# A hybrid mixer layer on one core: the passage from the output projection to the up products rebuilt, weight sums of three pairs made in memory, down products issued by parts

## The chip, the cores and the metric

One core of a Trainium2 chip runs the whole layer in one launch. The metric is the device time of one execution in microseconds (us). The engines are TensorE (PE in the profile), VectorE (DVE), ScalarE (ACT), GpSimd (POOL) and SyncE (SP, which issues DMAs; POOL issues some too). Each engine works through its own instructions in order.

## The reference, cut to what matters

The layer runs over 640 tokens: 512 denoising tokens and 128 context tokens, 1024 features each, with adaLN scale and shift (`sc2`, `sh2`) that differ between the two sets. What the change touches is its second half:

```
x = x + g1 * (merged @ w_o)
h = rmsnorm(x, norm2_g) * (1.0 + sc2) + sh2
z = dwconv3(h @ w_up, cw, cb)            # w_up: 1024 x 5632
a, g = split(z, 2)
x = x + g2 * ((silu(g) * a) @ w_down)    # w_down: 2816 x 1024
```

followed by a final `rmsnorm`. All of it is float32. The kernel splits each operand into a rounded high part and a low rest (`hi`, `lo`), and one product becomes three matmuls: high by high, high by low and low by high.

## The kernel before, in words

The up and the down products use a seven-product form of a 2 x 2 block product. The operand `h` is cut in two token halves (c = 0, 1, 320 tokens each) and two feature halves (q = 0, 1, 512 features each): a11, a12 (c = 0), a21, a22 (c = 1). The weights of one *pair* (a 128-column tile of each half of `w_up`; there are 22 pairs) have four blocks b11, b21, b22, b12. The products are numbered 1 to 7: 1 and 2 use a11 and a12 as they are; 5, 6 and 7 use a21 - a22, (a21 - a22) - a11 and a11 - a21; 4 uses a22; 3 uses a12 + (operand 6). On the weight side, three sums of blocks (`S0`, `S1`, `S2`) go with 6 or 5 or 7, a fourth sum (`S3`) with product 4 and b22 with product 3. One product is 12 matmuls of 128 x 128 by 128 x 320 (4 chunks of 128 features, three parts each).

*The passage.* `wo_tile` makes the output projection tile by tile. After its last tile it takes the statistics of half 0, normalises (`normed`), adds the shift (`shifted`), and splits into high and low (`part`), for the feature halves in turn. `up_all` then starts the pairs 0 to 3 (`BRIDGE = 4`) with their products 1 and 2, which need half 0 only, and beside them does half 1: statistics (`stats_a` to `stats_d`), `normed` and `shifted` of both feature halves, and then `operands()`, which forms the operands of products 5, 6, 7, 4 and 3, one after the other on VectorE (differences and low parts) and ScalarE (high parts, line 138 in the profile, as for every engine wrapped by `Ordered`). Then `up_pair(0)` to `up_pair(22)` run as a pipeline: `up_pair(p)` makes products 6, 5 and 7 of pair p and 4 and 3 of pair p - 1, the convolution and the gate of pair p - 2 (`taps`, `gate`, `gated`, `keep`), and prepares the weights of pair p + 1 (`up_ah`/`up_al` for b11 and b21, `up_sums`, `up_b`/`up_bl`, and in the next pair `up_c`).

*Buffers.* Raw weights wait in a pool of three tiles (`rp`, tag `raw`); from pair 3 on, the second half of an odd pair goes to the region `G`. Half 1 lies in the region `X1`, half 0 in `XL1`; the operands go to `B`, `A`, `D`, `XL0` and `XL1`. The low parts of S3 and b22 are made by `low_dma`: ScalarE writes the negated high part and a DMA of GpSimd's queue adds the raw block to it.

*The down part.* `down_all` works through 42 groups (7 products by 6 chunks) of 24 matmuls (12 for the last chunk). Each needs `w_hi`, `w_lo`, `x_hi` and `x_lo` of its group; group i's are prepared some groups ahead.

*What sets the order.* With `fixed[0]` set, the instructions of VectorE, ScalarE and GpSimd that go through `ovec`, `oact` and `opool` keep the program's order. Matmuls and SyncE's DMAs are not held: a planner orders them at compile time by its own costs. Generators put in with `start` are stepped along as the program issues matmuls (`tick`); `up_early` and the sums of `w_down` in memory (`weight_sums`) run beside earlier stages.

Of the kernel before, what the change touches and what calls it, by code (L numbers as in the profile page):

```python
# [57 lines left out]
def tile_step(ctx: ExitStack, tc: tile.TileContext, a: dict, outs: list, dbg=None):  # L58
# [1112 lines left out]
    axs = [None]  # L1171
    x2d = dram.tile([2, P, 4, T], F32, name="x2d")
    KO = ((0, 1, 4, 5), (2, 3, 6, 7))
    HOLD = 5
# [67 lines left out]

    def shifted(c, q, on_vec):
        f = hh[c][:, q]
        for k in range(4):
            for (t0, t1, v) in pieces(c):
                x, sh = f[:, k, t0:t1], modt[:, 24 + 4 * q + k, v:v + 1]
# [25 lines left out]
    def wo_tile(n, w):  # L1273
# [152 lines left out]

    def up_b(p_):
        s = sums(p_)
        b = up[p_, "B"] = unit(p_, 1)
        c = up[p_, "C"] = unit(p_, 2)  # L1430
        oact(b[:, 0:2], s[:, 0:2], AF.Copy)
        oact(b[:, 4], s[:, 2], AF.Copy)
        return b, c

    def up_bl(p_):
        s, b, c = sums(p_), up[p_, "B"], up[p_, "C"]
        ovec.tensor_tensor(b[:, 2:4], s[:, 0:2], b[:, 0:2].bitcast(F32), ALU.subtract)
        ovec.tensor_tensor(c[:, 4], s[:, 2], b[:, 4].bitcast(F32), ALU.subtract)

    def up_c(p_, r):  # L1440
        c = up[p_, "C"]
        for i, x in enumerate((sums(p_)[:, 3 + p_ % 2], r[1][:, 0])):
            oact(c[:, i], x, AF.Copy)
            low_dma(c[:, 2 + i].rearrange("p b c -> p (b c)"), x.rearrange("p b c -> p (b c)"))

    def prod(o, p_, i, first, part=None):

        u, ih, il = PROD[i]
        wh = up[p_, u][:, ih]
        wl = up[p_, "C" if i == 7 else u][:, il]  # L1450
        xh_, xl_ = fx["x"][i]
        for k in range(4) if part is not None else ():
# [101 lines left out]
    def up_pair(p_, r):  # L1554
# [4 lines left out]
        if p_ == 0:  # L1559
            prod(up[p_, "b"][1], p_, 5, True)  # L1560
            up_u2(p_)
            first_sum(2)
        if o >= 0:
            taps(o, 1)
        if q >= 0:

            oact(tmp(2), up[q, "b"][0], AF.Copy)
            for (i0, i1, c) in S2:
                ovec.tensor_tensor(ubuf(q, 1)[:, c:c + i1 - i0], up[q, "b"][1][:, i0:i1], tmp(2)[:, i0:i1],
                                  ALU.subtract)  # L1570
# [6 lines left out]
        if o >= 0:  # L1577
# [5 lines left out]
        if inner and p_:  # L1583
            up_c(p_, r[p_])
        if o >= 0:
            keep(o)
        if inner:
            if p_ + 2 < NPAIR:
                r[p_ + 2] = up_load(p_ + 2)
            elif p_ + 2 == NPAIR:  # L1590
                down_start(0)
        else:
            prep([1], [1])
        if q >= 0:
# [7 lines left out]
            if p_ == 1:  # L1602
                first_copy(3)
                first_sum(3)
        if inner and p_:
            up_u2(p_)
        if q >= 0:

            prod(up[q, "b"][1], q, 3, False)
            ovec.tensor_tensor(ubuf(q, 1)[:, 1:1 + HC], up[q, "b"][1], tmp(q % 2), ALU.subtract)  # L1610
        if nx:
            up_b(n)
        if not inner:
            prep([2], [])
        if q >= 0:
            centre(q, 1)
        if not inner:
            prep([], [2])
        if nx:
            up_bl(n)  # L1620
        if inner:
            b1, b2 = up[p_, "b"]
            if p_:
# [5 lines left out]
    def operands():  # L1629
        t = region("X0", [P, 2, 4, HC])  # L1630
        t5, t6 = t[:, 0], t[:, 1]
        a11, a12, a21, a22 = [hh[c][:, q] for c in range(2) for q in range(2)]
        x4, x6, x5, x7 = [region(t_, [P, 2, 4, HC], F32R) for t_ in ("XL0", "A", "B", "D")]
        fx["x"].update({i: (x[:, 0], x[:, 1]) for i, x in ((6, x6), (5, x5), (7, x7), (4, x4))})

        def lo(x, v):
            ovec.tensor_tensor(x[:, 1], v, x[:, 0].bitcast(F32), ALU.subtract)

        ovec.tensor_tensor(t5, a21, a22, ALU.subtract)
        oact(x5[:, 0], t5, AF.Copy)  # L1640
        ovec.tensor_tensor(t6, t5, a11, ALU.subtract)
        oact(x6[:, 0], t6, AF.Copy)
        lo(x5, t5)
        ovec.tensor_tensor(a21, a11, a21, ALU.subtract)
        oact(x7[:, 0], a21, AF.Copy)
        lo(x6, t6)
        oact(x4[:, 0], a22, AF.Copy)
        lo(x7, a21)
        ovec.tensor_tensor(t5, a12, t6, ALU.add)
        lo(x4, a22)  # L1650
        x3 = region("XL1", [P, 2, 4, HC], F32R)
        oact(x3[:, 0], t5, AF.Copy)
        lo(x3, t5)
        fx["x"][3] = x3[:, 0], x3[:, 1]

    def up_all(_):
# [4 lines left out]
        r = {1: up_load(1)}  # L1661
        up_sums(1, r[1], 0)
        up_sums(1, r[1], 1)
        fixed[0] = True
# [4 lines left out]
        for p_ in range(BRIDGE):  # L1669
# [6 lines left out]
            if p_ == 0:  # L1676
                stats_a(1, g[0][:, 1])
                dg = stats_b(1, g[0][:, 1])
            if p_ == 1:
                stats_c(dg, g[1][:, 1])  # L1680
                for q in range(2):
                    normed(1, q, g[1][:, 1])
                shifted(1, 0, False)
                shifted(1, 1, True)
# [5 lines left out]
        operands()  # L1690
        for p_ in range(NPAIR + 1):
            up_pair(p_, r)
        taps(NPAIR - 1, 1)
        gate(NPAIR - 1)
# [96 lines left out]
    def prep(iw, ix):  # L1791
        for f, l in ((w_hi, iw), (x_sum, ix), (w_lo, iw), (x_hi, ix), (x_lo, ix)):
            for i in l:
                f(i)

# [12 lines left out]
    def group_mm(o, i, js):  # L1808
        p_, g = GR[i]
        w, s = slots["w", i], slots["x", i]  # L1810
        for kk in range(many(g)):
            k = 2 * g + kk
            for j in js:
                for q, (h, x) in enumerate(((0, 0), (0, 1), (1, 0))):
                    mm(o[j], w[:, h, kk, j * P:(j + 1) * P], s[:, x, kk, :],  # L1815
                       start=(p_ in STARTS and k == 0 and q == 0), stop=(k == 10 and q == 2),
                       skip_group_check=True)
                tick(0.44)

# [413 lines left out]
```

## Time and profile before

| | us |
|---|---|
| median of 3 runs | 1040.14 (1038.79 to 1040.32) |
| profiled execution, its time | 1039.98 |
| its span, first to last instruction | 1038.2 |
| PE busy in the span | 1016.9 (98%) |
| DVE, ACT, POOL busy | 824.9, 541.3, 129.9 |

The profiled execution lies 0.16 us below the median. 1.8 us of its time lie outside the span. PE is busy in 98% of the span and not busy for 21.3 us of it.

### The profile page before, as it was taken

How to read it: one execution, taken by the hardware profiler on the slowest of the kernel's cores; microseconds unless marked ns; L12 is line 12 of the kernel's file. 1: busy time of each engine (PE TensorE's matmuls, PEld its weight loads, DVE VectorE, ACT ScalarE, POOL GpSimd, SP SyncE). 2: the span in 40 equal slices, each digit the busy share in tenths (PEclk: the TensorE clock that was granted, in tenths of full speed). 3: DMA queues.
4: the chain of work that ended last, by engine and by line, in shares of the span. 5: the costliest groups of instructions: out<-in, count | busy, mean ns of one | idle time of the engine just before them, and what ended most of it. 6: DMA issues, size and time to landing. Idle time of an engine off the chain costs nothing. (4 is left out here: it accounts for less than half of the span.)

```text
span 1038.2 us, 19770 instructions
## 1 busy us (share of the span) xinstructions
PE 1016.9 (98%) x8020; PEld 989.7 (95%) x8020; DVE 824.9 (79%) x1333; ACT 541.3 (52%) x926; POOL 129.9 (13%) x195
## 2 busy tenths in 40 slices
PE   8999999999999999999999998999999999999996
PEld 6899989998899999999999988999999999899996
DVE  5658899789878677767669578998888886998775
ACT  6532343342332554445446357777777776655663
POOL 2000010201100011111110001222222222000000
PEclk9999989999999999999999999999999999999998
DMA  9854443464154277898778652765565657976732
GB/s 362 325 198 127 128 136 123 133 217 130 54 201 179 89 236 203 259 257 231 199 222 318 255 178 68 195 167 148 149 157 159 160 154 210 355 266 183 226 92 102
DMA packets 64541, 196.00 MB, mean 189 GB/s; under 512 B 9121, under 2 KB 22049, under 8 KB 61121
## 3 DMA queue, kind: packets, MB, share of 16 engines
q1 hardware_dynamic: 49008, 149.08, 41.4%
q0 software_dynamic: 15440, 45.65, 19.1%
q8 instruction: 63, 1.03, 0.4%
q14 instruction: 30, 0.24, 0.1%
HBM read 160.72 MB, written 44.56 MB: 198 GB/s over the span
## 5 line engine op out<-in xcount | busy, mean ns | idle before, releaser
L305 PE MATMUL g<-XH,w 128*128 128x320 f32 x832 | 202.7, 319 | 0.0
L305 PEld LDWEIGHTS g<-XH,w 128*128 128x128 f32 x832 | 144.0, 191 | 2.6 <-issue 1.4
L305 PE MATMUL g<-XL,w 128*128 128x320 f32 x416 | 130.5, 314 | 0.0
L305 PEld LDWEIGHTS g<-XL,w 128*128 128x128 f32 x416 | 79.4, 191 | 0.8 <-issue 0.7
L138 ACT ACTIVATE w<-F 128x1024 fp32r<-128x1024 f32 (+1 forms) x65 | 49.0, 788 | 23.7 <-issue 18.0
L270 ACT ACTIVATE w<-raw 128x1024 fp32r<-128x1024 f32 (+1 forms) x34 | 37.8, 1113 | 36.2 <-PE g L305 14.0
L271 DVE TENSOR_TENSOR w<-raw,w 128x1024 fp32r<-128x1024 f32 (+1 forms) x34 | 43.7, 1285 | 8.1 <-ACT w L270 7.9
L138 DVE TENSOR_TENSOR w<-F,w 128x1024 fp32r<-128x1024 f32 (+1 forms) x43 | 41.9, 997 | 8.1 <-ACT w L138 7.8
L1056 PE MATMUL m<-XH,w 128*128 128x320 f32 x192 | 45.1, 310 | 0.0
L1815 PE MATMUL m<-XH,w 128*128 128x320 f32 x264 | 41.4, 312 | 1.7 <-DVE XH L138 0.9
L138 DVE SCALAR_TENSOR_TENSOR X<-MG,p2t,X 128x641 f32<-128x641 f32 x44 | 38.9, 884 | 5.0 <-ACT X L138 4.1
L138 DVE TENSOR_TENSOR w<-S,w 128x1024 fp32r<-128x1024 f32 (+1 forms) x32 | 32.2, 1021 | 13.3 <-ACT w L138 12.4
L138 ACT ACTIVATE w<-S 128x1024 fp32r<-128x1024 f32 (+1 forms) x32 | 28.0, 894 | 26.7 <-issue 12.5
L1815 PEld LDWEIGHTS m<-XH,w 128*128 128x128 f32 x264 | 38.9, 188 | 2.8 <-DVE XH L138 1.4
L938 POOL DMA_DIRECT2D wsum<-in_w_down_dram x24 | 19.9, 903 | 160.2 <-DMA wsum<-in_w_down_dram 95.3
L138 DVE SCALAR_TENSOR_TENSOR X<-X,p2t,X 128x641 f32<-128x641 f32 x44 | 38.9, 884 | 1.0
L1815 PE MATMUL m<-XL,w 128*128 128x320 f32 x264 | 39.6, 309 | 0.0
L1459 PE MATMUL g<-XL,C 128*128 128x320 f32 x240 | 38.6, 309 | 0.4 <-ACT MG L138 0.4
L1815 PEld LDWEIGHTS m<-XL,w 128*128 128x128 f32 x264 | 38.9, 188 | 0.0
L1459 PE MATMUL g<-XL,w 128*128 128x320 f32 x240 | 38.7, 310 | 0.0
L1459 PEld LDWEIGHTS g<-XL,C 128*128 128x128 f32 x240 | 36.0, 188 | 0.7 <-ACT MG L138 0.7
L1459 PEld LDWEIGHTS g<-XL,w 128*128 128x128 f32 x240 | 35.9, 188 | 0.4 <-ACT MG L138 0.3
(552 smaller groups left out, 2808.4 us busy)
## 6 DMA issues: line engine op xcount, KB each, us to landing
raw<-in_w_up_dram SPq DMA_DIRECT2D x32, 512.0 KB, 5.1
raw<-in_w_gp_dram SPq DMA_DIRECT2D x18, 640.0 KB, 6.9
wsum<-in_w_down_dram POOLq DMA_DIRECT2D x20, 512.0 KB, 7.9
raw<-in_w_in_dram SPq DMA_DIRECT2D x19, 512.0 KB, 4.4
H<-in_w_adt_dram SPq DMA_DIRECT2D x14, 512.0 KB, 4.2
actd<-X POOLq DMA_DIRECT2D x22, 256.0 KB, 4.2
raw<-in_w_gate_dram SPq DMA_DIRECT2D x8, 640.0 KB, 4.0
wsum<-in_w_down_dram SPq DMA_DIRECT2D x10, 512.0 KB, 7.0
```

Source lines behind the costliest of these rows:

```text
L138: r = f(*args, **kw)
L270: act(w[:, 0], raw, AF.Copy)
L271: low = lambda: vec.tensor_tensor(w[:, 1], raw, w[:, 0].bitcast(F32), ALU.subtract)
L305: mm(o, w[:, h, k0 + k, :], r(k)[:, s], start=(k == 0 and i == 0), stop=(k == kt - 1 and i == 2))
L938: tc.keep_in_program_order(eng.dma_start(o, x, **kw))
L1056: mm(o, w[:, k, :], x[:, k, :], start=(first and k == 0 and j == 0), stop=(k == 3 and j == 2), skip_group_check=True)
L1459: mm(o, w[:, k, :], x[:, k, :], start=(first and k == 0 and j == 0), stop=(k == 3 and j == 2), skip_group_check=True)
L1815: mm(o[j], w[:, h, kk, j * P:(j + 1) * P], s[:, x, kk, :], start=(p_ in STARTS and k == 0 and q == 0), stop=(k == 10 and q == 2), skip_gro ...
```

## The change

Four edits belong together. (1) *Half 1 is normalised as a difference.* While the statistics of half 1 are on their way, VectorE subtracts the scaled halves (`diff`); after that `normed` of the first feature half gives a21 - a22 at once, with the difference of the shifts (`dsh`, made once) added. The operands are then formed in place by a generator, `operands(m)`, whose steps are called between the products. (2) *A new order* in `up_all` and in `up_pair` 0 to 2; the shifts of half 0 go half to VectorE and half to ScalarE, those of a22 to ScalarE; products of pairs 0 and 1 issue all four high-by-high matmuls first. (3) *Weight sums of pairs 1 to 3 are made in memory* by `up_sums_ahead`, 24 DMAs of 256 KB (12 of SyncE, 12 adding ones of GpSimd), started after the input projection's section `du`; `up_load` of these pairs fetches the sums, and their `up_sums` fall away. (4) *Down products by parts*: a group issues high by high, then low weights, then low operand, and group 3's high parts are prepared before the last convolution.

The core of the diff (left out: signatures, `down_start`, moved lines of `up_pair` that only mirror others):

```diff
+            if sec == "du":
+                start(up_sums_ahead(), 6)
...
+    def up_sums_ahead():
+        b11, b21, b22, b12 = [a["w_up"][1:BRIDGE, h, :, i] for h in range(2) for i in range(2)]
+        s = [usum[:, :, 4 * i:4 * i + 4] for i in range(4)]
...
+        for steps in (((nc.sync, 0, b11), (nc.sync, 2, b12)), ((pool, 0, b12), (pool, 2, b22)),
+                      ((nc.sync, 1, s[0]),), ((pool, 1, b22),), ((nc.sync, 3, s[1]),), ((pool, 3, b21),)):
+            for eng, i, x in steps:
+                put(eng, s[i], x, **({"accum_op": ALU.add} if eng is pool else {}))
+            yield 12
...
         for q in range(2):
             normed(0, q, rb)
-            shifted(0, q, False)
+            shifted(0, q, (0, 1), True)
+            shifted(0, q, (2, 3), False)
+        for q in range(2):
             part(xw[:, 2 * q], xw[:, 2 * q + 1], hh[0][:, q])
...
     def up_load(p_):
+        if p_ < BRIDGE:
+            u = usum[p_ - 1].rearrange("p (i k) c -> p i k c", i=4)
+            r = [rp.tile([P, 2, 4, P], F32, tag="raw", name=nm("raw")) for _ in range(2)]
+            nc.sync.dma_start(r[0], u[:, 0:2])
+            nc.sync.dma_start(r[1][:, 1], u[:, 2])
+            nc.sync.dma_start(sums(p_)[:, 3 + p_ % 2], u[:, 3])
+            nc.sync.dma_start(r[1][:, 0], a["w_up"][p_, 1][:, 0])
+            return r
...
+        if p_ < 2:
+            for j, (w, x) in enumerate(((wh, xh_),) + (((wl, xh_), (wh, xl_)), ((wh, xl_), (wl, xh_)))[p_]):
+                for k in range(4):
+                    mm(o, w[:, k, :], x[:, k, :], ...)
...
     def up_pair(p_, r):
+        if q >= 0:
+            u = tmp(2) if q else gp.tile([P, HC], F32, tag="gt", name=nm("u"))
+            oact(u, up[q, "b"][0], AF.Copy)
...
+            if q == 0:
+                up_c(1, r[1], (0,))
+                up_u2(1)
+                up_c(1, r[1], (1,))
+                next(fx["op"])
+                up_bm(1, r[1])
+                next(fx["op"])
+        if o == 0:
+            first_copy(3)
+            first_sum(3)
         if o >= 0:
             taps(o, 1)
...
-        if nx and p_:
+        if nx and n >= BRIDGE:
             up_sums(n, r[n], 0)
             up_sums(n, r[n], 1)
...
+            if p_ == 1:
+                up_b(2, r[2])
+                up_bl(2, r[2])
             centre(q, 0)
-            taps(q, 0)
+            if p_ > 1:
+                taps(q, 0)
+        if o == 0:
+            gate(0)
+            gated(0)
+            keep(0)
...
+    def diff(ks):
+        a, b = hh[1][:, 0, ks[0]:ks[-1] + 1], hh[1][:, 1, ks[0]:ks[-1] + 1]
+        ovec.tensor_tensor(a, a, b, ALU.subtract)
+
+    def operands(m):
+        (a11, a12), (t5, a22) = [[hh[c][:, q] for q in range(2)] for c in range(2)]
+        t6, t7 = a11, t5
+        normed(1, 0, m)
+        shifted(1, 0, (0, 1), True, dsh)
+        shifted(1, 0, (2, 3), False, dsh)
+        normed(1, 1, m)
+        l5 = operand(5, t5, "B")
+        yield
+        shifted(1, 1, range(4), False)
+        ovec.tensor_tensor(t6, t5, a11, ALU.subtract)
+        l6 = operand(6, t6, "A")
+        l5()
+        yield
+        ovec.scalar_tensor_tensor(t7, t6, -1.0, a22, ALU.mult, ALU.subtract)
+        l7 = operand(7, t7, "D")
+        l6()
+        l4 = operand(4, a22, "XL0")
+        l7()
+        l4()
+        yield
+        ovec.tensor_tensor(t5, a12, t6, ALU.add)
+        yield
+        l3 = operand(3, t5, "XL1")
+        l3()
+        yield
...
+                diff(range(3))
+                stats_s(1, g[0][:, 1])
+                diff((3,))
+                dg = stats_d(1)
...
             up_pair(p_, r)
+        prep_head()
         taps(NPAIR - 1, 1)
...
+    def prep_head():
+        for f in (w_hi, x_sum, x_hi):
+            f(HEAD)
...
-        for kk in range(many(g)):
-            k = 2 * g + kk
-            for j in js:
-                for q, (h, x) in enumerate(((0, 0), (0, 1), (1, 0))):
+        for q, (h, x) in enumerate(((0, 0), (1, 0), (0, 1))):
+            for kk in range(many(g)):
+                k = 2 * g + kk
+                for j in js:
```

`operand(n, x, tag)` writes the high part of operand n at once (ScalarE) and returns the call that makes its low part (VectorE). `up_bm` is the last line of the old `up_bl` (the low part of S2).

## Rows read from the trace of the kernel before

**Rows 1.** Stages: busy us of each engine (instructions), granted clock, DMA share, GB/s
```profile
140.00:240.00 100.00, 99.99 (x927) 94.71 (x926) 85.80 (x180) 40.17 (x89) 13.39 (x14) 0.97 0.48 151
600.00:643.00 43.00, 36.97 (x234) 35.21 (x233) 35.33 (x48) 27.17 (x49) 3.79 (x18) 0.96 0.39 121
```

**Rows 2.** Waits of PE, whole span: waiter, releaser: total us, times, longest
```profile
PE g L1459 <- ACT MG L138: 3.1, 2, 2.6
...
PE g L1459 <- DVE B L138: 1.2, 1, 1.2
...
PE g L1459 <- DVE XH L138: 1.0, 1, 1.0
PE m L1815 <- DVE XH L138: 0.9, 2, 0.5
PE g L1459 <- DVE A L138: 0.8, 1, 0.8
PE m L1815 <- ACT XH L138: 0.6, 1, 0.6
```

**Rows 3.** Stages of 2 us in the passage, columns as in rows 1
```profile
630.00:632.00 2.00, 2.00 (x9) 2.00 (x9) 2.00 (x3) 0.95 (x2) 0.29 (x7) 0.50 0.00 0
```

**Rows 4.** Order of time, PE: start, us, instruction, count, idle before and releaser
```profile
620.60 0.42 PE L1459 MATMUL g<-B,E 128*128 128x320 f32 x1
...
629.54 0.65 PE L1459 MATMUL g<-D,E 128*128 128x320 f32 x2 [2.64 <-ACT MG L138]
...
642.43 1.92 PE L1459 MATMUL m<-A,E 128*128 128x320 f32 x12
```

**Rows 5.** Order of time, DVE and ACT in the passage
```profile
612.58 2.88 DVE L138 TENSOR_TENSOR X<-X,g 128x1280 f32<-128x1280 f32 x2 [0.92 <-PE g L1226]
...
614.10 2.67 ACT L138 ACTIVATE X<-X,modt 128x192 f32<-128x192 f32 x8 [2.56 <-DVE X L138]
615.50 1.79 DVE L138 TENSOR_SCALAR X<-X,modt 128x192 f32<-128x192 f32 x8
...
619.26 1.28 ACT L138 ACTIVATE B<-X 128x1280 fp32r<-128x1280 f32 x1 [2.17 <-DVE X L138]
...
627.89 1.27 ACT L138 ACTIVATE XL<-X 128x1280 fp32r<-128x1280 f32 x1 [1.80 <-DVE X L138]
629.06 0.42 ACT L138 ACTIVATE MG<-g 128x320 f32<-128x320 f32 x1
```

**Rows 6.** Groups by form, 603 to 660: instruction, count, busy us, mean ns
```profile
L138 DVE SCALAR_TENSOR_TENSOR X<-MG,p2t,X 128x641 f32<-128x641 f32 x5 | 4.4, 886 | 1.8 <-ACT X L138 1.6
...
L138 DVE TENSOR_TENSOR X<-XL,X 128x1280 f32<-128x1280 f32 x2 | 3.0, 1486 | 0.0
...
L138 DVE TENSOR_TENSOR w<-F,w 128x1024 fp32r<-128x1024 f32 x2 | 2.4, 1216 | 0.0
...
L138 DVE TENSOR_TENSOR F<-F,raw 128x512 f32<-128x512 f32 x5 | 3.4, 687 | 0.1
```

**Rows 7.** Order of time, ACT and PE at pairs 2 to 4
```profile
643.09 1.28 ACT L138 ACT_TABLE_LOAD   x1
...
644.48 0.74 ACT L138 ACTIVATE X<-X 128x641 f32<-128x641 f32 x1
...
652.13 1.05 ACT L138 ACTIVATE MG<-raw 128x1024 fp32r<-128x1024 f32 x1
...
658.69 0.60 PE L1459 MATMUL g<-XH,MG 128*128 128x320 f32 x3
659.13 1.92 PE L1459 MATMUL m<-D,w 128*128 128x320 f32 x12
```

**Rows 8.** DMA issues, 590 to 660: tile, queue, count, KB each, median us to landing
```profile
raw<-in_w_up_dram SPq DMA_DIRECT2D x5, 512.0 KB, 5.0
...
C<-raw POOLq DMA_DIRECT2D x1, 256.0 KB, 5.9
```

**Rows 9.** Order of time, ACT where the down part begins
```profile
895.64 0.74 ACT L138 ACTIVATE X<-X 128x641 f32<-128x641 f32 x1 [2.61 <-DVE X L138]
```

More of the change, by code (lines that the diff above doesn't have):

```diff
@@ L929, in tile_step, with flat, put @@
     wsum = dram.tile([4, P, 11, 512], F32, name="wsum")
+    usum = dram.tile([BRIDGE - 1, P, 16, P], F32, name="usum")
+    def up_sums_ahead():
+        b11, b21, b22, b12 = [a["w_up"][1:BRIDGE, h, :, i] for h in range(2) for i in range(2)]
+        s = [usum[:, :, 4 * i:4 * i + 4] for i in range(4)]
+        def flat(x):
+            return [x[i].rearrange("p a b -> p (a b)") for i in range(BRIDGE - 1)]
+        def put(eng, dst, src, **kw):
+            for d, x in zip(flat(dst), flat(src)):
+                eng.dma_start(d, x, **kw)
+        for steps in (((nc.sync, 0, b11), (nc.sync, 2, b12)), ((pool, 0, b12), (pool, 2, b22)),
[3 more added lines that the diff above has]
+            yield 12
     def weight_sums(g):
@@ L1172, in tile_step @@
     x2d = dram.tile([2, P, 4, T], F32, name="x2d")
+    dsh = const.tile([P, 4, 2], F32, name="dsh")
     KO = ((0, 1, 4, 5), (2, 3, 6, 7))
@@ L1241, in normed, with shifted @@
         ovec.tensor_tensor(f, f, m[:, 0:HC].unsqueeze(1).to_broadcast([P, 4, HC]), ALU.mult)
-    def shifted(c, q, on_vec):
+    def shifted(c, q, ks, on_vec, col=None):
         f = hh[c][:, q]
-        for k in range(4):
+        for k in ks:
             for (t0, t1, v) in pieces(c):
-                x, sh = f[:, k, t0:t1], modt[:, 24 + 4 * q + k, v:v + 1]
+                x, sh = f[:, k, t0:t1], modt[:, 24 + 4 * q + k, v:v + 1] if col is None else col[:, k, v:v + 1]
                 if on_vec:
@@ L1305, in wo_tile @@
         xw = hh["w"] = region("XH", [P, 4, 4, HC], F32R)
+        vec.tensor_tensor(dsh, modt[:, 24:28], modt[:, 28:32], ALU.subtract)
         sm, rb = pm(), pm()
@@ L1374, in tile_step, with summands @@
     upd = dram.tile([4, P, 5, 4, P], F32, name="upd")
+    def summands(p_, r):
+        s = sums(p_)
+        return (r[0], r[1][:, 1]) if p_ < BRIDGE else (s[:, 0:2], s[:, 2])
     def up_early():
@@ L1425, in up_sums, with up_b, up_bl, up_bm @@
             ovec.tensor_tensor(s[:, 3 + p_ % 2], s[:, 1], b21, ALU.add)
-    def up_b(p_):
-        s = sums(p_)
+    def up_b(p_, r):
+        s01, s2 = summands(p_, r)
         b = up[p_, "B"] = unit(p_, 1)
         c = up[p_, "C"] = unit(p_, 2)
[L1431 to L1440, printed above, removed]
+        oact(b[:, 0:2], s01, AF.Copy)
+        oact(b[:, 4], s2, AF.Copy)
+    def up_bl(p_, r):
+        s01, b = summands(p_, r)[0], up[p_, "B"]
+        ovec.tensor_tensor(b[:, 2:4], s01, b[:, 0:2].bitcast(F32), ALU.subtract)
+        if p_ > 1:
+            up_bm(p_, r)
+    def up_bm(p_, r):
+        s2, b, c = summands(p_, r)[1], up[p_, "B"], up[p_, "C"]
+        ovec.tensor_tensor(c[:, 4], s2, b[:, 4].bitcast(F32), ALU.subtract)
+    def up_c(p_, r, js=(0, 1)):
         c = up[p_, "C"]
-        for i, x in enumerate((sums(p_)[:, 3 + p_ % 2], r[1][:, 0])):
+        for i in js:
+            x = (sums(p_)[:, 3 + p_ % 2], r[1][:, 0])[i]
             oact(c[:, i], x, AF.Copy)
@@ L1456, in prod @@
                 tick(0.147)
+        if p_ < 2:
+            for j, (w, x) in enumerate(((wh, xh_),) + (((wl, xh_), (wh, xl_)), ((wh, xl_), (wl, xh_)))[p_]):
+                for k in range(4):
+                    mm(o, w[:, k, :], x[:, k, :], start=(first and k == 0 and j == 0),
+                       stop=(k == 3 and j == 2), skip_group_check=True)
+                    tick(0.147)
+            return
         for k in range(4) if part is None else ():
@@ L1576, in up_pair @@
             first_sum(p_)
-        if o >= 0:
+        if not inner:
+            prep([1], [1])
+        if o > 0:
             gate(o)
             gated(o)
-        if nx and p_:
+        if nx and n >= BRIDGE:
             up_sums(n, r[n], 0)
             up_sums(n, r[n], 1)
-        if inner and p_:
+        if inner and p_ > 1:
             up_c(p_, r[p_])
-        if o >= 0:
+        if o > 0:
             keep(o)
@@ L1591, in up_pair @@
                 down_start(0)
-        else:
-            prep([1], [1])
         if q >= 0:
@@ L1599, in up_pair @@
                 oact(ubuf(q, 0)[:, c:c + i1 - i0], c1[:, i0:i1], AF.Copy)
+            if p_ == 1:
+                up_b(2, r[2])
+                up_bl(2, r[2])
             centre(q, 0)
-            taps(q, 0)
[L1602 to L1605, printed above, removed]
+            if p_ > 1:
+                taps(q, 0)
[3 more added lines that the diff above has]
+            keep(0)
+        if inner and p_ > 1:
             up_u2(p_)
         if q >= 0:
+            if p_ == 1:
+                prod(up[1, "b"][1], 1, 5, True)
             prod(up[q, "b"][1], q, 3, False)
             ovec.tensor_tensor(ubuf(q, 1)[:, 1:1 + HC], up[q, "b"][1], tmp(q % 2), ALU.subtract)
-        if nx:
-            up_b(n)
+        if nx and p_ != 1:
+            up_b(n, r[n])
         if not inner:
             prep([2], [])
+        if p_ == 1:
+            taps(0, 0)
         if q >= 0:
@@ L1618, in up_pair @@
             prep([], [2])
-        if nx:
-            up_bl(n)
+        if nx and p_ != 1:
+            up_bl(n, r[n])
         if inner:
             b1, b2 = up[p_, "b"]
-            if p_:
+            if p_ > 1:
                 prod(b2, p_, 5, True)
@@ L1627, in up_pair, with operand @@
             down_start(1)
[L1629 to L1640, printed above, removed]
-        ovec.tensor_tensor(t6, t5, a11, ALU.subtract)
[L1642 to L1648, printed above, removed]
-        ovec.tensor_tensor(t5, a12, t6, ALU.add)
[L1650 to L1654, printed above, removed]
+    def operand(n, x, tag):
+        r = region(tag, [P, 2, 4, HC], F32R)
+        fx["x"][n] = r[:, 0], r[:, 1]
+        oact(r[:, 0], x, AF.Copy)
+        return lambda: ovec.tensor_tensor(r[:, 1], x, r[:, 0].bitcast(F32), ALU.subtract)
+    def diff(ks):
[11 more added lines that the diff above has]
+        shifted(1, 1, range(4), False)
+        ovec.tensor_tensor(t6, t5, a11, ALU.subtract)
+        l6 = operand(6, t6, "A")
[8 more added lines that the diff above has]
+        yield
+        ovec.tensor_tensor(t5, a12, t6, ALU.add)
+        yield
+        l3 = operand(3, t5, "XL1")
+        l3()
+        yield
     def up_all(_):
@@ L1661, in up_all @@
         r = {1: up_load(1)}
-        up_sums(1, r[1], 0)
-        up_sums(1, r[1], 1)
         fixed[0] = True
@@ L1677, in up_all @@
                 stats_a(1, g[0][:, 1])
-                dg = stats_b(1, g[0][:, 1])
+                diff(range(3))
+                stats_s(1, g[0][:, 1])
+                diff((3,))
+                dg = stats_d(1)
             if p_ == 1:
                 stats_c(dg, g[1][:, 1])
[L1681 to L1684, printed above, removed]
+                fx["op"] = operands(g[1][:, 1])
+                next(fx["op"])
                 up_back(0, "B", unit(0, 1), 2, 5)
@@ L1689, in up_all @@
                 first_sum(p_)
-        operands()
+            if p_ == 1:
+                next(fx["op"])
+        next(fx["op"])
         for p_ in range(NPAIR + 1):
             up_pair(p_, r)
+        prep_head()
         taps(NPAIR - 1, 1)
@@ L1707, in tile_step @@
     FIRST_BANKS = (1, 6, 7, 4)
+    HEAD = 3
     X_DMA = [(p_, g) for p_ in (6, 3, 7) for g in (3, 5)]
@@ L1793, in prep @@
             for i in l:
-                f(i)
+                if i != HEAD or f not in (w_hi, x_sum, x_hi):
+                    f(i)
+    def prep_head():
+        for f in (w_hi, x_sum, x_hi):
+            f(HEAD)
     def down_start(part_):
```

10 lines of the change are left out of this document (4 added, 6 removed).

## The prediction

> **What bounds the kernel now.** I read the table of the profile first: PE is busy 98% of the span, so nothing is won by making another engine faster as such; only PE's gaps count. The view of stages says where they lie: between 600 and 643 us PE is busy 36.97 of 43, a gap of 6.0 us, while from 140 to 240 it is busy 99.99 of 100 [rows 1]. The view of waits names them: in the up part PE waited 3.1 us for ACT (one wait of 2.6), 1.2 and 0.8 for the low parts of operands 5 and 6, 1.0 for the low part of half 0; in the down part 0.9 and 0.6 in three waits [rows 2]. A second loss hides in busy time: after the long wait the granted clock is 0.50 for a stretch of 2 us, the 1.2 GHz level [rows 3].
>
> The order of time shows why. A matmul here takes 0.147 us (three from 658.69 to 659.13 [rows 7]). Product 5 of pair 0 begins at 620.60, product 6 of pair 2 at 642.43 [rows 4]; between them lie eight products, 96 matmuls, 14.1 us of work in 21.8 us. So 7.7 us are lost there: 5.1 of shown waits and some 2.6 at the low clock, and 1.0 more earlier. The 2.64 wait [rows 4] is an ordering matter: ACT copies product 6 out of its bank at 629.06, right behind the high part of operand 3 (627.89) [rows 5], which nothing needs before product 3. ACT works in order, so the copy, and with it product 7, stood behind an operand needed later.
>
> **The change part by part.** *Difference first.* Half 1's statistics arrive as before: DVE starts to normalise at 612.58 [rows 5]. Before, the path to product 5 was two normalisations, shifts, one subtraction, one high part, to 619.26 + 1.28 = 620.5 [rows 5]. The subtraction (1.49 [rows 6]) now lies in DVE's wait for the statistics; cover gone, it would cost 1.5. Then: normalise 612.6 to 614.0; four shifts on ACT (half of 2.67) to 615.5, four on DVE (half of 1.79) to 614.9 [rows 5]; high part 5 to 616.7. PE wants it at 619.7, if the 1.0 wait in front shrinks to 0.1 (high and low-weight matmuls of pair 0 come first, 8 of 12). The path has 3 us to spare.
>
> *The rest of the operands*, at 1.49 per DVE step and 1.27 per ACT high part [rows 5, 6]. DVE: second normalisation to 616.4, a first sum of 0.5 (an estimate from ACT's 0.42 for the same shape [rows 5]) to 616.9, operand 6 to 618.3, low 5 to 619.8, operand 7 as a scalar-tensor-tensor. The trace has none of that length; between 1.49, a plain subtraction, and 2 x 0.886 = 1.77 [rows 6] I take the latter, its own operation: 621.6. Then low 6 to 623.1, low 7 to 624.6, low 4 to 626.1. ACT: eight shifts (2.67) 616.7 to 619.4, high 6 to 620.7, a copy, high 7 to 622.9, high 4 to 624.1, the copy of product 6 to 624.5.
>
> PE: product 5 from 619.7 to 621.5 without a wait (low 5 is there at 619.8 and wanted 8 matmuls in). Product 6: eight matmuls to 622.6, waits for low 6 until 623.1, ends 623.7. Product 7 needs the copy: waits until 624.5, 0.8 us; behind it in order nothing else is ready, since pair 1's sums are rounded by ACT after that copy. Then pair 1's product 6 may wait 0.3 for its low sums (DVE: 626.1 + 0.5 + 1.22 = 627.8 [rows 6]), products 4 and 5 run, operand 3 (1.49 + 0.69 for a low sum + 1.49 on DVE [rows 6]) is complete at 632.7, when product 3 is in its last third. Waits: 0.1 + 0.5 + 0.8 + 0.3 = 1.7 us, none long; rows 2's waits of 0.8 to 1.2 ahead of the long one came without a low clock, so I charge none. Eight products end at 619.7 + 14.1 + 1.6 = 635.4 or 635.5 instead of 642.43: **6.9 us** won. Bounds: all the 8.7 us lost, or, if the planner keeps its former order of matmuls and one 2.6 wait with its low clock stays, half of that, 4.
>
> *Sums in memory.* They take 12 DVE additions of 0.69 [rows 6] off pairs 1 to 3, 8.3 us, of which pairs 2 and 3 (5.5) lie in this stage, where DVE is busy 35.3 of 43 [rows 1]. Their 24 DMAs start after section `du`, early in the stretch from 140 to 240, where the DMA engines are at 0.48 and PE is full [rows 1]. GpSimd's adding DMA of 256 KB lands in 5.9 us [rows 8] and steps are 12 apart; SP's copies behind it wait a little at most. I take 0; bound above 5.9, one weight load of SP standing behind one such wait uncovered.
>
> *What comes late next.* Pairs 1 to 3 now hold two raw tiles each, pair 3 too, which had `G` for its second. So pair 4's first weights can be fetched only once a raw tile of pair 2 or 3 is free: pair 2's is, when GpSimd's DMA has read b22. By my chain ACT ends pair 2's copies near 639.0: product 7 of pair 1 ends at 635.5, then come its copy and a first copy (0.42 each [rows 5]) and four copies of 512 columns, some 0.55 each (an estimate from 1.27 for 1280). The DMA takes 5.9, the fetch 5.0 [rows 8]: 650.2. Before, ACT rounded them at 652.13 [rows 7]. Only 1.9 us earlier, while PE is 6.9 ahead: ACT stands still, and behind it in order are the gate of pair 1, the copies of pair 3's sums and the copy of its product 6. Before, pair 3's product 7 (659.13) came 7.0 after that rounding [rows 7], so now not before 657.2. PE can meanwhile do pair 4's products 1 and 2, of which 3 matmuls were already ahead [rows 7]; the other 21 are 3.1 us. The gain kept is thus between 1.9 and 5.0; I take 4.5, near the upper end, since the planner used this very filling before: **2.4 us given back** (bounds 0, if the fetch is 2 us quicker, and 5.0).
>
> ACT's gate of pair 0 loads a table, 1.28 us, and goes on at 644.48, 0.1 after the load's end [rows 7]. In the new order ACT needs 7.0 us from the end of pair 1's product 7 to the copy of pair 2's product 6 (copies, centre, this load, the gate), and PE has four products, 7.1 us, for that time: 0 by the rows. The Trainium skill (ScalarE: Activation LUTs, What ACT_TABLE_LOAD costs) counts a drain of 1.38 us on top of the 1.28; the trace shows the load and not the drain, and by the page this place would cost 1.4 and the sum would be 1035.4.
>
> *Down part.* With the low weights 8 matmuls (1.2 us) and the low operand 16 (2.3 us) into a group, the two waits for DVE (0.9) vanish. Group 3's high parts (ACT) go ahead of the silu of the last pair, where ACT sat idle 2.61 us [rows 9]: the 0.6 vanishes. **1.5 us** won; bounds 0 and 1.5. No matmul is added or removed. The output bank of a group's first column tile is complete 6 matmuls or 0.9 us later; its readers are spread over the next groups.
>
> *Sum.* 1039.98 - 6.9 + 2.4 - 1.5 = 1033.98, the profiled execution's own time; the median before lies 0.16 above that, within its spread. I predict 1034.0.
>
> **The rivals.** (A) *Slower: the fetch of pair 4's weights stops PE.* If pair 2's copies end 8 us after my 639.0, because ACT is held up in front of them, pair 4's rounding starts at 658.2, 6.1 after 652.13; the filling covers 3.1, the down part 1.5, the low clock after so long a wait adds some 2.6: 1039.98 + 6.1 - 3.1 - 1.5 + 2.6 = 1044. It decides once rounding starts after 656.7 (652.13 + 3.1 + 1.5). For it: the chain of DMA, fetch, rounding is serial. Against it: pair 2's sums need no DVE work now. Chance 0.10. (B) *ACT and DVE become the bound*: the fetch as forecast, but no filling, pair 5 late too: 1.9 kept and 1.0 to 1.5 of the down part, 1036.5 to 1038. Against it: after the passage both have idle time. Chance 0.18. (C) *Everything is kept*: 1039.98 - 6.9 - 1.5, 1031.6, down to 1030 if the other waits vanish. Chance 0.10. (D) *The change doesn't do what it says*: the planner orders matmuls anew so that the waits only move, 1039 to 1041. Chance 0.05. (E) *The sums in memory hold up the input projection* by one landing, 5.9: 1040. Chance 0.04. (F) *The table load keeps the copy of pair 2's product 6* by 1.4 more: 1035.4, inside the forecast's range. The rows show no pause after the load: 0.03. (The page named above would have it so.)
>
> **How the numbers follow.** The forecast, 1031.5 to 1036.5, has 0.53 with F. A measurement tells 0.2%, 2.1 us, from no change. Faster by more: the forecast, C and nearly all of B, 0.80. Within: D, half of E, the rest of B, 0.10. Slower: A and little else, 0.10. The range reaches from 1030.5 to 1039.0: forecast, B and the greater part of C.
>
> **What would show it.** Right: DVE subtractions at 608 to 610, ahead of the normalisation; high part 5 by 617; no wait of PE over 1 us until product 6 of pair 2, which begins near 635.5; a granted clock of 1.00 there; no waits of PE in the down part for high or low operands. Half right: PE waiting at pairs 3 to 5, with ACT idle for a DMA into `raw` before it rounds pair 4's weights. Wrong: a new wait of PE over 2.6 us with a clock of 0.50 behind it; PE under 99% in 140 to 240; or pair 4's rounding after 656.7.

## The result and the profile after

After the change the kernel takes 1044.15 us (median of 20 runs), beside 1040.40 before on the same chip: ratio 1.0034, interval 1.0019 to 1.0048. It is slower by 3.7 us, where 6 us of gain were forecast. The profiled execution took 1046.06, with a span of 1044.3 and PE busy for 1016.3. Four of the medians further down hold one execution each that took far longer than the rest (1102 to 3469 us: before_sums, before_down, held_g, and the kernel before on the chip of the last three); the ratios leave these out.

The waits of PE come first (waiter, releaser: total us, times, longest).

```profile
PE g L854 <- ACT MG L352: 10.3, 1, 10.3
...
PE m L1507 <- ACT X L138: 1.4, 1, 1.4
...
PE g L1501 <- ACT MG L138: 0.5, 1, 0.5
...
PE g L1501 <- DVE A L138: 0.3, 1, 0.3
```

The passage's waits (L1459 in [rows 2], L1501 and L1507 now) have shrunk, and the waits of the down part (L1815 there) are gone. On top stands a wait of 10.3 at line 854, which is in the input projection, some 500 us ahead of the passage, in a stretch for which the prediction had a price in its rival E alone. The view of stages around it (us, PE, PEld, DVE, ACT, POOL busy, granted clock, DMA share, GB/s):

```profile
60.00:100.00 40.00, 40.00 (x304) 39.89 (x303) 19.84 (x25) 11.75 (x16) 8.04 (x10) 1.00 0.81 186
...
105.00:110.00 5.00, 2.61 (x22) 2.40 (x21) 0.00 (x0) 0.00 (x0) 0.84 (x2) 1.00 1.03 300
110.00:115.00 5.00, 0.00 (x0) 0.00 (x0) 4.74 (x8) 0.00 (x0) 0.00 (x0) 0.72 0.75 185
115.00:120.00 5.00, 2.14 (x10) 2.14 (x11) 5.00 (x8) 2.28 (x3) 0.00 (x0) 0.50 0.49 176
120.00:125.00 5.00, 5.00 (x106) 4.82 (x106) 4.96 (x10) 0.00 (x0) 0.00 (x0) 0.76 0.44 149
```

PE stands still for 10 us, and DVE does nothing from 105 to 110. The clock then is 0.50, the 1.2 GHz level: 2.14 us of work at half speed and five at 0.76 lose 1.1 and 1.2 more. In the kernel before the same 20 us held 19.91 of PE at 1.00; its first and third five of them:

```profile
105.00:110.00 5.00, 5.00 (x44) 5.00 (x43) 3.74 (x6) 0.98 (x2) 0.00 (x0) 1.00 0.33 113
...
115.00:120.00 5.00, 4.91 (x85) 4.33 (x87) 5.00 (x9) 2.68 (x9) 0.00 (x0) 1.00 0.60 196
```

Who is late is seen on SP's own queue, in order of time (start, us, instruction, count):

```profile
74.41 8.43 SPq L943 DMA_DIRECT2D usum<-usum  x2
82.92 0.54 SPq L281 DMA_DIRECT2D raw<-in_w_tok_dram  x1
83.92 15.52 SPq L943 DMA_DIRECT2D usum<-usum  x3
99.96 0.33 SPq L263 DMA_DIRECT2D raw<-in_w_in_dram  x1
100.38 0.48 SPq L943 DMA_DIRECT2D usum<-usum  x1
100.95 0.64 SPq L212 DMA_DIRECT2D H<-in_w_adt_dram  x1
```

Before, that load of a column of `w_adt` into H was issued at 84.25:

```profile
84.25 0.33 SPq L212 DMA_DIRECT2D H<-in_w_adt_dram  x1
```

Now all six copies from sum to sum stand ahead of it. SP's waits between 60 and 130 us, and then those of the other engines, give the chain:

```profile
SPq L943 <- DMA usum<-in_w_up_dram: 24.9, 5, 7.4
```

```profile
POOL usum L943 <- DMA usum<-in_w_up_dram: 33.0, 3, 25.4
POOL usum L943 <- DMA usum<-usum: 24.1, 5, 10.5
DVE junk L225 <- DMA H<-in_w_adt_dram: 19.0, 1, 19.0
ACT E L435 <- DVE B L486: 18.6, 1, 18.6
```

GpSimd adds a block and SP's copies wait for it, five times and 24.9 us in all. SP's column load stands behind them; DVE, whose column products (line 225) keep the program's order, waits 19.0 for it; ACT waits for DVE, and PE for ACT's evacuation. All 24 DMAs of the sums were issued between 62 and 108 us. The program calls `start` behind section `du`, but nothing holds these DMAs, and the planner put them far ahead: where they are held (below), the first starts at 150.1.

In the passage, order of time, PE and then ACT:

```profile
616.78 1.44 PE L1501 MATMUL g<-XH,MG 128*128 128x320 f32 x8
...
632.67 1.92 PE L1501 MATMUL g<-B,E 128*128 128x320 f32 x12
...
636.10 0.85 PE L1501 MATMUL g<-A,E 128*128 128x320 f32 x4 [0.34 <-DVE A L138]
637.49 0.85 PE L1501 MATMUL g<-D,E 128*128 128x320 f32 x4 [0.54 <-ACT MG L138]
...
648.19 1.92 PE L1507 MATMUL m<-A,E 128*128 128x320 f32 x12
...
667.41 0.85 PE L1507 MATMUL m<-D,w 128*128 128x320 f32 x4 [1.38 <-ACT X L138]
...
1035.82 0.55 PE L1937 MATMUL m<-cst,last 128*128 128x128 f32 x3
```

```profile
653.68 1.28 ACT L138 ACT_TABLE_LOAD   x1
654.97 0.74 ACT L138 ACTIVATE X<-X 128x641 f32<-128x641 f32 x1
...
661.94 1.06 ACT L138 ACTIVATE MG<-raw 128x1024 fp32r<-128x1024 f32 x1 [3.30 <-DMA raw<-in_w_up_dram]
```

Four instructions are good marks: the first matmul of the up part (line 1459 before, 1501 after), product 6 of pair 2 and product 7 of pair 3 [rows 4, 7], and the last matmul. Between marks a stage is read whatever came ahead of it. The table gives them for the profiled execution of each kernel (the last five columns are experiments, below):

| us | before | after | held | held_g | no_sums | before_down | passage_only |
|---|---|---|---|---|---|---|---|
| first matmul of the up part | 603.57 | 616.78 | 605.48 | 603.23 | 604.96 | 603.46 | 608.64 |
| to product 6 of pair 2 | 38.86 | 31.41 | 31.39 | 31.41 | 31.71 | 38.01 | 31.71 |
| from there to product 7 of pair 3 | 16.70 | 19.22 | 18.86 | 17.69 | 20.66 | 16.70 | 20.67 |
| from there to the last matmul | 370.63 | 368.41 | 368.39 | 367.45 | 367.32 | 368.58 | 368.80 |

So the changed kernel enters the up part 13.2 late, wins 7.45 in the passage, gives 2.5 back and wins 2.2 by the end: 13.2 - 7.45 + 2.5 - 2.2 = 6.1, the difference of the two profiled executions. The one after lies 1.9 above its median and the one before 0.4 below, so the medians differ by 3.7 only.

### The profile page after: what moved, and what is told of

Its sections match the earlier page's. It is cut to its first block, busy times and chain, and to the rows that moved or that the text cites. A ratio compares the mean times of both kernels' runs of the same rounds, so it can differ in the third digit from the quotient of the medians.

```text
span 1044.3 us, 19800 instructions
## 1 busy us (share of the span) xinstructions
PE 1016.3 (97%) x8020; PEld 989.5 (95%) x8020; DVE 816.0 (78%) x1323; ACT 540.0 (52%) x926; POOL 141.9 (14%) x207
## 3 DMA queue, kind: packets, MB, share of 16 engines
q8 instruction: 63, 1.03, 0.4%
## 4 chain that ended last, share of the span: by engine, by line
PE 80%; DVE 9%; DMA 6%; issue 2%; ACT 1%; SPq 0%; POOL 0%; DVEq 0%; POOLq 0%; ACTq 0%
PE g L1507 18%; PE g L305 14%; PE m L1076 14%; PE m L1901 6%; PE g L1901 6%; PE m L1281 4%; PE g L1089 4%; PE m L1507 3%; DMA usum<-in_w_up_dram 2%; PE g L1501 2%; PE g L138 2%; PE m L138 1%; DVE junk L225 1%; PE g L1281 1%; DMA B<-in_w_ada_dram 1%
## 5 line engine op out<-in xcount | busy, mean ns | idle before, releaser
L305 PE MATMUL g<-XL,w 128*128 128x320 f32 x416 | 129.9, 312 | 0.0
L305 PEld LDWEIGHTS g<-XL,w 128*128 128x128 f32 x416 | 78.9, 190 | 0.8 <-issue 0.7
L138 ACT ACTIVATE w<-F 128x512 fp32r<-128x512 f32 (+1 forms) x61 | 45.8, 783 | 19.0 <-issue 17.7
L138 DVE TENSOR_TENSOR w<-F,w 128x1024 fp32r<-128x1024 f32 (+1 forms) x39 | 38.3, 1002 | 6.7 <-ACT w L138 6.5
L854 PE MATMUL g<-w,XH 128*128 128x256 f32 x128 | 28.0, 304 | 10.3 <-ACT MG L352 10.3
L1507 PE MATMUL g<-XL,C 128*128 128x320 f32 x216 | 34.7, 309 | 0.0
L1507 PE MATMUL g<-XL,w 128*128 128x320 f32 x216 | 34.7, 309 | 0.0
L138 ACT ACTIVATE X<-X,p2t 128x641 f32<-128x641 f32 (+1 forms) x29 | 24.0, 837 | 17.7 <-DVE X L138 17.6
```

Source lines behind the costliest of these rows:

```text
L138: r = f(*args, **kw)
L305: mm(o, w[:, h, k0 + k, :], r(k)[:, s], start=(k == 0 and i == 0), stop=(k == kt - 1 and i == 2))
L854: mm(o, x(kx)[:, ts], w[:, h, k, :], start=(kx == 0 and i == 0), stop=(kx == 7 and i == 2))
```

## The experiments

Theory Q: SP's queue stands behind copies that wait for GpSimd. Theory T: 24 more DMAs fill the DMA engines (share 0.81 from 60 to 100, 1.03 from 105 to 110, above), and loads land late in whatever queue. Theory P: the loss is elsewhere, in the new passage or the down part. Medians and ratios to the kernel before on the same chip:

| kernel | median | ratio, 95% interval |
|---|---|---|
| sp_no_wait | 1034.92 | 0.9954 (0.9936 to 0.9971) |
| pool_copies | 1035.16 | 0.9959 (0.9944 to 0.9975) |
| held | 1034.46 | 0.9943 (0.9925 to 0.9962) |
| no_sums | 1033.83 | 0.9947 (0.9928 to 0.9966) |
| before_sums | 1049.87 | 1.0112 (1.0094 to 1.0131) |
| before_down | 1037.21 | 0.9981 (0.9972 to 0.9990) |
| passage_only | 1035.12 | 0.9973 (0.9955 to 0.9990) |
| held_g | 1030.53 | 0.9925 (0.9911 to 0.9939) |
| after_g | 1040.30 | 1.0012 (0.9995 to 1.0029) |
| held_again | 1033.75 | 0.9944 (0.9925 to 0.9963) |
| held_g_again | 1031.55 | 0.9914 (0.9894 to 0.9934) |

The first four ran on one chip (before: 1039.08), the next four on one (1039.27), the last three on one (1039.52).

**sp_no_wait: the same traffic, without SP's waits.**

```diff
-                      ((nc.sync, 1, s[0]),), ((pool, 1, b22),), ((nc.sync, 3, s[1]),), ((pool, 3, b21),)):
+                      ((nc.sync, 1, b11),), ((pool, 1, b22),), ((nc.sync, 3, b12),), ((pool, 3, b21),)):
```

> The six copies of S1 and S3 read their raw block (b11, b12) instead of the sum, so SP does not wait for GpSimd's adding DMAs; the sums S1 and S3 of pairs 1 to 3 therefore lack one or two blocks. Traffic, place and the order of PE, DVE and ACT are those of the changed kernel. Theory Q (SP's queue stands behind the copies): SP's 24.9 us of waits go, the column loads of w_adt are issued some 10 us earlier, DVE's wait of 19 falls under 6, PE's wait of 10.3 under 2, time 1031 to 1034. Theory T (traffic: 24 more DMAs fill the DMA engines at 60 to 110 us): the loads still land in 9 to 12 us, half of the wait or more stays, 1038 to 1044. Theory P (the loss is the passage's or the down part's): 1043 to 1045.

SP's queue and the stage from 60 to 100 in this kernel:

```profile
84.97 0.33 SPq L212 DMA_DIRECT2D H<-in_w_adt_dram  x1
```

```profile
60.00:100.00 40.00, 40.00 (x303) 39.89 (x302) 21.94 (x28) 12.02 (x16) 10.14 (x12) 1.00 0.97 249
```

SP's waits for DMAs into the sums fall from 24.9 to 1.1 us. The column load is issued at 84.97 again, though the DMA engines are fuller than in the changed kernel (0.97 against 0.81). The wait at line 854 is gone, and the time falls by some 9 us by medians and 8 by the ratios. DVE still waits 7.9 for columns (under 6 was expected): with SP free, this is put down to traffic (loads into H land in 5.6 us here and in 3.8 in the kernel before, medians from 60 to 130). Q holds; T explains a wait of DVE, not the loss; P is out.

**pool_copies: the copies go to GpSimd's queue** (left out: the line that keeps them from adding).

```diff
-                      ((nc.sync, 1, s[0]),), ((pool, 1, b22),), ((nc.sync, 3, s[1]),), ((pool, 3, b21),)):
+                      ((pool, 1, s[0]),), ((pool, 1, b22),), ((pool, 3, s[1]),), ((pool, 3, b21),)):
```

> The six copies go to GpSimd's queue, behind the adding DMAs that they need; nothing else moves. Theory Q: SP waits for none of them, the wait of 10.3 goes, 1031 to 1034. Theory T: the same bytes in the same stretch, a little thinner since GpSimd waits in order: the wait is 5 or more, 1038 to 1044. A third way: GpSimd's queue is now behind by some 30 us, and the memset and copies of hgrn that stand behind it in order delay the section: 1036 to 1044 with DVE or PE waiting for POOL.

The same sums are made in the same stretch (share 0.92 from 60 to 100), and 1035.16 is what sp_no_wait gives. DVE's waits for columns are 3.8 and 3.5, PE's at line 854 none. The copies do no harm on a queue on which nothing urgent stands behind them; the third way, GpSimd's own work late, did not show.

**held: the DMAs keep the program's order.**

```diff
-                eng.dma_start(d, x, **kw)
+                tc.keep_in_program_order(eng.dma_start(d, x, **kw))
```

> All 24 DMAs keep the program's order, and so start after section du, near 150 us, where the prediction had put them. Order of PE, DVE and ACT unchanged. Theory Q: SP still waits for GpSimd, now at 150 to 230, where the loads behind it have more time in hand: PE's wait in the input projection is under 2, time 1031 to 1034, at most 1036. Theory T says the same from the lower DMA share there (0.48 before). Theory P: 1043 to 1045. If a wait of some 6 us stands in 150 to 260, the rival of the prediction (one landing uncovered) was right in kind and only the place wrong: 1037 to 1039.

Uses of `usum` in this kernel (operation, count: duration, first and last start), and pair 4's rounding:

```profile
L943 POOL DMA_DIRECT2D usum<-in_w_up_dram x12: 814/984/1214, 155.8 to 213.7; - x12
L943 SPq DMA_DIRECT2D usum<-in_w_up_dram x6: 551/596/641, 150.1 to 153.2; - x6
L943 SPq DMA_DIRECT2D usum<-usum x6: 482/547/548, 176.1 to 206.9; - x6
```

```profile
650.25 1.06 ACT L138 ACTIVATE MG<-raw 128x1024 fp32r<-128x1024 f32 x1 [2.93 <-DMA raw<-in_w_up_dram]
```

At the place that the prediction had in mind PE loses at most 0.4 us to the 24 DMAs, which are issued from 150 to 214 us: it is busy for 59.59 of 60 us from 140 to 200, and for 60.00 of 60 from 200 to 260.

```profile
140.00:200.00 60.00, 59.59 (x644) 56.16 (x644) 52.33 (x116) 25.94 (x57) 17.31 (x17) 0.98 0.78 212
```

DVE's waits for columns from 130 to 300 us sum to 1.6, and between 140 and 230 SP waits for none of GpSimd's DMAs, where Q expected it to wait still. Columns of `w_adt` pass through SP's queue there too, but the steps are now apart: the first adding DMAs are issued from 155.8 to 161.1, and the copies that need them at 176.1. In the changed kernel the copies stood right behind the adding DMAs. The whole change gives 1034.46. The rival's 1037 to 1039 did not come. The rounding at 650.25 still waits for the fetch.

**no_sums: no sums in memory.** Undoes edit 3 alone (`up_sums` of pairs 1 to 3 back on DVE, pair 3's second half in `G`; left out: the lines on the loads and on pair 1):

```diff
             if sec == "du":
-                start(up_sums_ahead(), 6)
+                pass
...
-        if nx and n >= BRIDGE:
+        if nx and p_:
             up_sums(n, r[n], 0)
```

> The sums of pairs 1 to 3 are made on DVE again as in the kernel before (12 additions of 0.69, and pair 3's second half in G again), the rest is the changed kernel. Theory Q and T both: the wait of 10.3 goes. With DVE's 5.5 us of additions back in the passage, the passage keeps between 3 and 7 of its 7.5 us, the fetch of pair 4 gives nothing back, the down part keeps 1.5 to 2.2: 1030 to 1036. Theory P: 1043 to 1045.

1033.83: the wait at line 854 is gone. The table of marks shows where the time goes with DVE's additions back: product 6 of pair 2 is little later (31.71), but product 7 of pair 3 comes 20.66 after it, and DVE is busy for 20.24 of these 20.66 us (15.54 of 17.69 in held_g, below).

**before_sums: the DMAs alone, in the kernel before.** `up_sums_ahead` and its start are added to the kernel before; no one reads `usum`.

> The kernel before with the 24 DMAs of the sums alone, started where the change starts them; nothing reads the result. SP's and GpSimd's order around 60 to 110 us is that of the changed kernel. Theory Q (SP's queue stands behind copies that wait for GpSimd): the whole loss appears without the new passage, DVE's wait for a column load near 19, PE's near 10, the low clock behind it, 12 to 14 us slower than before: 1051 to 1053. Theory P (the loss needs the new order of the passage or of the down part): within 2 us of before.

```profile
DVE junk L225 <- DMA H<-in_w_adt_dram: 16.7, 1, 16.7
...
PE g L854 <- ACT MG L352: 7.9, 1, 7.9
```

```profile
116.00:120.00 4.00, 4.00 (x20) 4.00 (x20) 4.00 (x10) 0.51 (x1) 0.00 (x0) 0.50 0.52 156
```

These are its waits between 60 and 130 us and the stage of 4 us behind them. It takes 1049.87, 10.6 over before by medians and 11.6 by the ratio (9.8 to 13.6), where 12 to 14 were expected; PE's wait is 7.9 and not 10.3. It enters the up part at 614.80, 11.2 later than before. The chain and the low clock behind it are there without a line of the new passage: the sums' DMAs are enough.

**before_down: edit 4 alone** (the group's loop by parts and `prep_head`, as in the diff above, in the kernel before).

> The kernel before with edit 4 alone: down products by parts, group 3's high parts ahead of the last convolution. The prediction's term is 1.5 (three waits of PE); the difference of the two traces from pair 3's product 7 to the end was 2.2. So 1.5 to 2.2 us faster than before, 1037 to 1037.6. If the 2.2 were a remainder of the passage, 0 to 1.

```profile
PE m L1822 <- DVE w L138: 0.3, 1, 0.3
```

That is the only wait of PE from 860 us on; the waits of 0.9 and 0.6 [rows 2], and one of 0.2 for a DMA, are gone. 2.1 us by medians (ratio 1.0 to 2.9), 2.05 by the marks.

**passage_only: edits 1 and 2 alone** (no_sums with the down products of before).

> Edits 1 and 2 alone: the changed kernel without the sums in memory and with the down products as before. With the additions of pairs 2 and 3 on DVE again (5.5 us in the passage). If the passage is not bound by DVE: it gains 5 to 7 us, no fetch is late (pair 3's second half is in G), 1032.5 to 1034.5. If DVE becomes the bound there, the sums in memory were needed for the gain: 1036 to 1038.

1035.12, 4.2 under before by medians and 2.8 by the ratio (1 to 4.7), between the two expectations. Its times scatter from 1034.3 to 1041.1 and the profiled one is 1040.36, with an entry into the up part at 608.64. Between marks its first two stages are those of no_sums (31.71 and 20.67). So the passage without the sums is worth some 3 to 5 us. The last stage is 1.48 longer than in no_sums, from which this kernel differs by edit 4 alone.

**held_g and after_g: pair 3's second half in `G`**, in `held` and in the changed kernel:

```diff
-            r = [rp.tile([P, 2, 4, P], F32, tag="raw", name=nm("raw")) for _ in range(2)]
+            r = [region("G", [P, 2, 4, P]) if p_ == 3 and i else rp.tile([P, 2, 4, P], F32, tag="raw", name=nm("raw")) for i in range(2)]
```

> The whole change, with the 24 DMAs held in the program's order (section du's end, 150 us) and the second half of pair 3's weights in G, as before the change, so that pair 4's fetch needs no raw tile of pair 2's b22. If the 2.4 us given back are that fetch: pair 4's rounding waits for no DMA, 1031.5 to 1033, some 2 us under the version with held DMAs alone. If ACT's own work sets pair 4's rounding (the prediction's rival B), 1034 to 1035, no better.

> The changed kernel as it is (DMAs of the sums at 62 to 108 us), with the second half of pair 3's weights in G alone. If the fetch of pair 4 costs what the traces say (rounding 3.3 us late, 2.5 given back), about 2 us under the changed kernel's 1044.15: 1041 to 1042.5, while the wait of 10 in the input projection stays. If something else in the passage sets pair 4's rounding: 1043.5 to 1044.5.

Order of time in held_g, ACT and PE:

```profile
644.99 1.05 ACT L138 ACTIVATE MG<-raw 128x1024 fp32r<-128x1024 f32 x1
```

```profile
634.64 1.92 PE L1507 MATMUL m<-A,E 128*128 128x320 f32 x12
...
652.33 1.92 PE L1507 MATMUL m<-D,w 128*128 128x320 f32 x12
```

Pair 4's rounding waits for no DMA now and comes 10.4 after product 6 of pair 2, where it was 13.4 in held. held_g is the fastest kernel of the study, 8.7 us under before by medians and 7.8 by the ratio. after_g keeps the wait at line 854 (7.3 in its profiled execution) and is 0.8 over before, where the changed kernel is 3.7 over it: 3 us less by medians, 2.3 by the ratios (1.0012 against 1.0034, with intervals that overlap), where about 2 were expected. Between marks its last two stages are those of held_g (17.69 and 367.48), 2.5 us less than in the changed kernel.

**held_again and held_g_again, side by side.**

> The version with held DMAs again, on the chip of the next one: 1034 to 1035, 4.6 us under before.

> The version with held DMAs and G again, beside the one without G. If G is worth the 2.4 us given back: 1.5 to 2.5 below its neighbour. If more (the first comparison, over two calls, showed 1034.5 against 1030.5): 3 to 4, and then something else than the fetch moved too.

held_again is 5.8 us under before by medians, where 4.6 were expected. `G` takes off 2.2 us more by medians, 3.1 by the ratios. The marks of both pairs of traces say 2.1 to 2.2, of which 1.2 to 1.3 lie ahead of pair 3's product 7 and 0.9 behind it. So `G` is worth 2 to 3; whether anything beside the fetch is in it stays open.

## Why the prediction was wrong

**The step that failed** is the paragraph on the sums in memory: "Their 24 DMAs start after section `du`, early in the stretch from 140 to 240 ... I take 0; bound above 5.9". Two things in it were wrong. The *place*: the section on what sets the order says that SyncE's DMAs are not held, and the prediction used this for matmuls only. The planner issued them from 62 us on, where `w_adt`'s columns come in for a DVE that keeps its order, and closer together than the steps of 12 that the prediction counted on. The *bound*: it counted one load behind one wait of 5.9. Six copies in a row depend on GpSimd's adding DMAs; they waited 24.9 together, and a load behind all of them was issued 16.7 late (100.95 against 84.25). The wait of 10.3 and the low clock behind it are what is left of that after the cover. Its price is 10.6 to 11.6 by before_sums and 9.4 by the ratios of the changed kernel and held (1.0034 against 0.9943). At the forecast place, with the steps apart, the term of 0 was nearly right: held shows no wait of SP for these DMAs there. Rival E had the mechanism, at one landing (1040) and a chance of 0.04; with the measured wait in place of one landing it would have given 1034 + 10 = 1044, the measured time. The mark that was named for it, PE under 99% from 140 to 240, looked at the wrong stretch; the other one, a wait over 2.6 with a clock of 0.50 behind it, showed it.

The Trainium skill (DMA: Bandwidth & Descriptors, Anatomy of one DMA) says that the DMA engines wait on no semaphores: a wait is held by the engine that issues the DMA. The trace agrees: the 24.9 us in five waits stand on SP's queue. In pool_copies SP has none of them, and GpSimd waits for DMAs from `w_up` into the sums eight times (43.9 us) where it did three times (33.0).

**The rest, by its own steps**, in held, where the DMAs lie as forecast: 1034.46 and 1033.75 against 1034.0. By the ratios that is 5.9 and 5.8 us of gain for 6.0. So close a number is in part luck: between the marks held gains 7.6, and its profiled execution enters the up part 1.9 later than the one before.

*Passage*: 7.5 measured for 6.9. In the changed kernel, less the 13.2 ahead of it, the high part of operand 5 ends at 617.0 and product 6 of pair 2 begins at 635.0 (616.7 and 635.5 forecast). Product 6 waits 0.34 for low 6 (0.5 forecast), product 7 waits 0.54 for the copy (0.8), no clock below 1.00. The scalar-tensor-tensor of operand 7 took 1.49, not the 1.77 chosen:

```profile
633.15 1.49 DVE L138 SCALAR_TENSOR_TENSOR X<-XL,X 128x1280 f32<-128x1280 f32 x1
```

One reading of the prediction here was wrong: the "some 2.6 at the low clock" is a remainder, not a measured price. before_down has the same passage and the same wait of 2.64, and its clock stays at 1.00:

```profile
629.42 0.56 PE L1459 MATMUL g<-D,E 128*128 128x320 f32 x2 [2.64 <-ACT MG L138]
...
629.96 0.45 PE L1459 MATMUL g<-D,E 128*128 128x320 f32 x2
```

Product 7 of pair 0 takes 1.9 us there (629.42 to 631.28) and 3.1 before (629.54 to 632.65), and the whole stage is 0.85 shorter, as it is in before_sums (38.01 too). So the clock cost some 1.2 there, not 2.6, and of the 7.45 won 0.85 belongs to that one execution of the kernel before: against the passages of before_down and before_sums the new one wins 6.6.

*Given back*: 2.4 forecast, 2.5 measured after the change, 2.2 in held. Mechanism and place were right: ACT is idle 2.93 for the DMA into `raw` before it rounds pair 4's weights, and product 7 of pair 3 comes behind it. held_g wins back 1.2 of it there and 0.9 behind product 7; of the 1.0 that it keeps PE is idle for 0.3. The two terms inside were off and made up for each other, which is luck. The sum up to the rounding gives 649.9 (639.0 + 5.9 + 5.0) and not 650.2. The rounding at 650.25 in held looks like a hit, but this execution is 1.9 late at the first mark: counted from there the rounding comes at 648.3, 3.8 ahead of before and not 1.9. The filling in turn brought 1.5 and not 2.6, as product 7 came 5.5 behind the rounding and not 4.4.

*Down part*: 1.5 forecast; 2.05 measured by before_down in the old passage, above the upper bound, and 1.48 by passage_only and no_sums in the new one. The three waits were sized by the idle time that the view shows, and this leaves out a part: in the kernel before, four matmuls from 882.21 are recorded with 0.75 us, where four steps of 0.147 are 0.59, and the wait is shown only from there on. By the steps the three waits come to some 2.1 us (an estimate from the rows at 882, 890 and 898 us).

*Sums in memory* also had a gain that was put at nothing: with the DMAs held and `G` used, product 7 of pair 3 comes 17.69 after product 6 of pair 2, without them 20.66. They are worth 3.0 us there, and 3.1 from the first mark to the last. DVE, busy for 20.24 of 20.66 us without them, speaks for its additions as the cause; it is not shown alone, as the planner also orders the matmuls differently without the sums.

*Table load* (rival F): silu at 654.97 follows 0.01 after the load's end (653.68 + 1.28). The drain of the Trainium skill (ScalarE: Activation LUTs, What ACT_TABLE_LOAD costs) is not in the trace here either.

Of rivals A, B and D nothing showed; C needs `G` for its 1031.6: held_g gave 1030.53 and 1031.55.

## What to carry to other kernels

A transfer that is put "after" a stage in the program starts there only if something holds it: look in the rules of order for what holds each queue before costing its place, and cost a dependent chain by its length (six copies, 24.9 us), not by one landing. A DMA that must wait for another queue's result belongs on a queue on which nothing urgent stands behind it. When several edits come together, run each on its own: here a gain of some 6 us (held) was hidden under 9 to 10 us of one edit's side effect.

## What the runs showed of the hardware that was not expected

GpSimd's adding DMAs of 256 KB from memory to memory landed in 8.1 us (median) in the changed kernel and in 14.0 in sp_no_wait, where SP's copies ran beside them and the DMA share was 0.97, against 5.9 for the one from tile to tile [rows 8]. The changed kernel's group of DMA issues from 60 to 130:

```profile
usum<-in_w_up_dram POOLq DMA_DIRECT2D x12, 256.0 KB, 8.1
```

DVE's scalar-tensor-tensor of 1280 columns took as long as a subtraction of that size (1.49). And two profiled executions of the same kernel, held and held_again, entered the up part at 605.48 and 608.93, while their stages behind it agree within 0.2 us: stages between marks are a finer measure than whole times, as long as the granted clock in them is the same. Where it was not (the passage in before and in before_down, both with the wait of 2.64), the same stage differed by 0.85 us.
